# ff2 by seven block products in 12 of 16 chunks, with half of ff1's low parts from an accumulating transfer

## The chip, the cores and the metric

One core of a Trainium2 chip runs the kernel. The metric is the device time of one execution in microseconds. The engines named here: PE (matmuls), DVE (elementwise), ACT (activations, casts), POOL, and the queues that issue transfers, SP's and POOL's among them. Each works through its own list of instructions in order and waits on the others by semaphores.

## The reference, cut to what matters

One decoder layer on 256 tokens of width 1024, all in float32: a token mixer, then an MLP with squared ReLU, then a final norm. The change touches only the MLP:

```
h = rms_norm(x, norm_mlp)
u = square(relu(h @ w_ff1))     # w_ff1: 1024 x 4096
x = x + u @ w_ff2               # w_ff2: 4096 x 1024
return rms_norm(x, norm_final)
```

## The kernel before, in words

The kernel hands PE operands in a rounded format (`F32R`), so each float32 operand is split into a high part (`hi`, the rounded value) and a low part (`lo`, what is left), and each product is three matmuls: hi x hi, hi x lo, lo x hi (`mm3`). `split` (L70) does it: ACT casts to `hi`, DVE subtracts to get `lo`.

The weights come in chunks of 128 x 2048 floats (1 MB). `load` (L89) issues the transfer of a chunk into one of three `raw` buffers from SP's queue; `split_w` (L96) splits it, half by half, into one of four buffers for high parts (`wh`) and one of four for low parts (`wl`), and after the second half issues the load three chunks ahead. The hidden width 4096 is cut into NF = 16 groups j. Group j has one ff1 chunk (1024 x 256 of w_ff1) and one ff2 chunk (256 x 1024 of w_ff2); the chunks alternate: ff2's j, ff1's j+2, and so on.

`ff1` (L785) makes the 256 hidden values of a group for all 256 tokens in one PSUM bank: 2 halves x 8 steps over the width x 3 = 48 matmuls of 256 columns. `ff1_out` and `ff1_evac` (L772) then make r = relu (ACT), uh = r squared as high part (ACT), u = r squared (DVE), ul = u - uh (DVE). `ff2_mm` (L797) multiplies: a group's u is a 2 x 2 arrangement of 128 x 128 blocks (two halves kk of the hidden values, two halves t of the tokens), its ff2 chunk a 2 x 2 arrangement of 128 x 512 blocks (kk, and n for two halves of the output). Four banks `facc[t, n]` collect all groups; each group adds 2 kk x 4 (t, n) x 3 = 24 matmuls of 512 columns.

The whole program is one hand-written order: each engine issues its instructions as the code emits them. Until the MLP, a list of slots with a `plan` of side steps gives the order. Then a loop over j (L916) emits: ff2 of group j; the splits of the next ff1 chunk; ff1 of group j+2; the splits of the next ff2 chunk; the evacuation of group j+2. I call one pass of it a turn. The last two groups are left to a tail: `last_mm` (L942) runs both for one piece of the output after another, and the final norm and the stores follow piece by piece.

Of the kernel before, what the change touches and what calls it, by code (L numbers as in the profile page):

```python
# [32 lines left out]
def trunk_kernel(ctx: ExitStack, tc, x, x_t, w_in, w_out, w_ff1, w_ff2, small, hg_norm, norm_final, out):  # L33
    nc = tc.nc
    V, A, G, T = nc.vector, nc.scalar, nc.gpsimd, nc.tensor

    const = ctx.enter_context(tc.tile_pool(name="const", bufs=1))
    RAW = 3
    raw_p = ctx.enter_context(tc.tile_pool(name="raw", bufs=RAW))
    spl_p = ctx.enter_context(tc.tile_pool(name="spl", bufs=4))  # L40
# [38 lines left out]
    NF = 16  # L79
    chunks = [w_in[c] for c, _ in in_order] + [w_out[j] for j in range(4)]  # L80
# [536 lines left out]
    ps_s, sc_t, nm_t, pr_t, ps_t, PT = {}, {}, {}, {}, {}, {}  # L617
# [145 lines left out]
    FI = NI + 4  # L763
    uh, ul = {}, {}

    def ff1_mm(o, i, c, k):
        wh = hi_w[i].rearrange("p (k c) -> p k c", c=CW)
        wl = lo_w[i].rearrange("p (k c) -> p k c", c=CW)
        cs = slice(c * 128, (c + 1) * 128)
        mm3(o, (wh[:, k, cs], wl[:, k, cs]), (x1h[:, k, :], x1l[:, k, :]), k == 0, k == KT - 1)  # L770
# [12 lines left out]
    ff1_ps = {}  # L783

    def ff1(j, i):  # L785
        ps = ff1_ps[j] = mis(f"f{j}")
        for c in range(2):
            for k in range(KT):
                ff1_mm(ps[:, c * 256:(c + 1) * 256], i, c, k)

    def ff1_out(j):
        ff1_evac(j, [(ff1_ps[j], slice(0, 512))])
        free(f"f{j}")

    facc = {}

    def ff2_mm(j, i, kk, t, n):  # L797
        if j == 0 and kk == 0:
            facc[t, n] = mis(f"fo{t}{n}")
        cs = slice(kk * 256 + t * 128, kk * 256 + (t + 1) * 128)  # L800
        big_mm(facc[t, n], uh[j][:, cs], ul[j][:, cs], i, kk, n, j == 0 and kk == 0,
               (t, n) == (1, 1) and j == NF - 3 and kk == 1)

    f0 = {}

    def ff1_first(c, kg):
# [106 lines left out]
    i = FI + 2  # L913
# [150 lines left out]
```

## Time and profile before

| | us |
|---|---|
| median of 3 runs (lowest, highest) | 320.41 (320.21, 321.88) |
| the profiled execution | 320.52 |
| its span | 318.8 |
| PE / DVE / ACT busy in the span | 309.5 / 191.9 / 171.9 |

The span runs from the first to the last instruction of the profile; the execution's own time lies 1.7 us above it. Matmuls overlap in the records (each lasts longer than its distance to the next), so PE's prices are read from start to start.

### The profile page before, as it was taken

To read this page: it belongs to the slowest core of one execution; us is meant where nothing else is said; L and a number is where in the kernel's file an instruction comes from. 1 tells how busy PE (TensorE), PEld (TensorE's weight loads), DVE (VectorE), ACT (ScalarE), POOL (GpSimd) and SP (SyncE) were. 2 spreads that over 40 slices of the span, in tenths; PEclk is the share of its full clock that TensorE was granted. 3 is DMA by queue.
4 is the path that set the end of the run, shared out by engine and by line. 5 is a ranking of instruction groups with operands and counts; after the bars stand their busy time and mean duration, and the time that the engine had idled before them with its cause. 6 is when DMAs were issued, how large, how long until landed. Compare 5 with 4: busy or idle time off the path is not lost.

```text
span 318.8 us, 5290 instructions
## 1 busy us (share of the span) xinstructions
PE 309.5 (97%) x2164; PEld 283.4 (89%) x2164; DVE 191.9 (60%) x287; ACT 171.9 (54%) x283; POOL 34.2 (11%) x83
## 2 busy tenths in 40 slices
PE   7999999999999999999999999999999999999991
PEld 6999999998999888999899889889989988988881
DVE  1848999983545493697734743753573474366353
ACT  3869699684595460686632652562364265246131
POOL 8338600021410000000000000000000000000000
PEclk9999999999999999999999999999999999999997
DMA  7996553360046346058656246436525624630003
GB/s 202 411 387 229 177 222 132 134 243 23 2 148 249 133 141 257 0 199 329 217 246 255 88 185 264 140 125 265 205 85 238 263 85 181 263 134 1 0 5 129
DMA packets 9961, 55.71 MB, mean 175 GB/s; under 512 B 1232, under 2 KB 1488, under 8 KB 4048
## 3 DMA queue, kind: packets, MB, share of 16 engines
q1 hardware_dynamic: 9216, 54.06, 45.1%
q10 hardware_dynamic: 720, 1.31, 1.3%
q8 instruction: 17, 0.28, 0.3%
q14 instruction: 8, 0.07, 0.1%
HBM read 54.32 MB, written 1.05 MB: 174 GB/s over the span
## 4 chain that ended last, share of the span: by engine, by line
PE 87%; DVE 5%; ACT 2%; DMA 2%; issue 2%; POOLq 0%; POOL 0%; DVEq 0%; ACTq 0%
PE banks L301 26%; PE banks L303 26%; PE banks L302 26%; DVE wl L72 2%; DMA raw<-in_w_in_dram 2%; PE banks L405 2%; ACT wh L71 1%; PE banks L641 1%; PE banks L659 1%; PE banks L168 1%; PE banks L676 1%; PE banks L675 1%; PE banks L458 1%; PE banks L521 1%; PE banks L674 1%
## 5 line engine op out<-in xcount | busy, mean ns | idle before, releaser
L72 DVE TENSOR_TENSOR wl<-raw,wh 128x1024 fp32r<-128x1024 f32 (+1 forms) x100 | 113.8, 1184 | 19.3 <-ACT wh L71 17.7
L71 ACT CAST wh<-raw 128x1024 fp32r<-128x1024 f32 (+1 forms) x100 | 95.3, 1009 | 3.3 <-DMA raw<-in_w_in_dram 3.3
L301 PE MATMUL banks<-x1h,wh 128*128 128x256 f32 x256 | 72.4, 283 | 0.0
L302 PE MATMUL banks<-x1l,wh 128*128 128x256 f32 x256 | 72.4, 283 | 0.0
L303 PE MATMUL banks<-x1h,wl 128*128 128x256 f32 x256 | 72.4, 283 | 0.0
L778 ACT ACTIVATE fr<-banks 128x512 f32<-128x512 f32 (+1 forms) x17 | 9.7, 573 | 87.2 <-PE banks L303 87.2
L780 DVE TENSOR_TENSOR fu<-fr 128x512 f32<-128x512 f32 (+1 forms) x17 | 11.2, 659 | 69.5 <-ACT fr L778 69.5
L303 PE MATMUL banks<-wh,ul 128*128 128x512 f32 (+1 forms) x132 | 51.4, 390 | 0.1
L301 PE MATMUL banks<-wh,uh 128*128 128x512 f32 (+1 forms) x132 | 51.4, 390 | 0.0
L302 PE MATMUL banks<-wl,uh 128*128 128x512 f32 (+1 forms) x132 | 51.4, 389 | 0.0
L301 PEld LDWEIGHTS banks<-x1h,wh 128*128 128x128 f32 x256 | 49.0, 191 | 0.7
L302 PEld LDWEIGHTS banks<-x1l,wh 128*128 128x128 f32 x256 | 48.9, 191 | 0.7
L303 PEld LDWEIGHTS banks<-x1h,wl 128*128 128x128 f32 x256 | 49.0, 191 | 0.0
L301 PE MATMUL banks<-hTh,wh 128*128 128x256 f32 x128 | 37.5, 293 | 0.3 <-ACT hTh L161 0.3
L302 PE MATMUL banks<-hTl,wh 128*128 128x256 f32 x128 | 36.4, 284 | 0.7 <-DVE hTl L162 0.7
L303 PE MATMUL banks<-hTh,wl 128*128 128x256 f32 x128 | 36.3, 283 | 0.0
L303 PEld LDWEIGHTS banks<-wh,ul 128*128 128x128 f32 x132 | 24.8, 188 | 6.2 <-DVE ul L781 0.6
L301 PEld LDWEIGHTS banks<-wh,uh 128*128 128x128 f32 x132 | 24.9, 189 | 5.4 <-ACT uh L779 0.4
L302 PEld LDWEIGHTS banks<-wl,uh 128*128 128x128 f32 x132 | 24.9, 188 | 5.0
L302 PEld LDWEIGHTS banks<-hTl,wh 128*128 128x128 f32 x128 | 24.5, 191 | 1.2 <-DVE hTl L162 1.1
L301 PEld LDWEIGHTS banks<-hTh,wh 128*128 128x128 f32 x128 | 24.5, 191 | 1.2 <-ACT hTh L161 0.7
L303 PEld LDWEIGHTS banks<-hTh,wl 128*128 128x128 f32 x128 | 24.5, 191 | 0.2 <-DVE wl L72 0.2
(198 smaller groups left out, 412.9 us busy)
## 6 DMA issues: line engine op xcount, KB each, us to landing
raw<-in_w_ff_dram SPq DMA_DIRECT2D x32, 1024.0 KB, 5.1
raw<-in_w_in_dram SPq DMA_DIRECT2D x10, 1024.0 KB, 5.7
raw<-in_w_out_dram SPq DMA_DIRECT2D x4, 1024.0 KB, 4.8
raw<-in_w_in_dram ACTq DMA_DIRECT2D x4, 256.0 KB, 7.1
xtok<-in_x_dram SPq DMA_DIRECT2D x2, 512.0 KB, 8.0
xa<-in_x_dram SPq DMA_DIRECT2D x2, 512.0 KB, 6.2
xa<-in_x_t_dram SPq DMA_DIRECT2D x3, 256.0 KB, 6.2
raw<-in_w_in_dram SPq DMA_DIRECT2D x2, 256.0 KB, 8.0
```

Source lines behind the costliest of these rows:

```text
L71: A.copy(hi, src)
L72: V.tensor_tensor(lo, src, hi.bitcast(F32), op=OP.subtract)
L168: T.transpose(pair[n % 2][:, i * 256 + t * 128:i * 256 + (t + 1) * 128], src[:, t, (k0 + n) * P:(k0 + n + 1) * P], ident)
L301: T.matmul(o, lh, rh, start=first, stop=False)
L302: T.matmul(o, lh, rl, start=False, stop=False)
L303: T.matmul(o, ll, rh, start=False, stop=last)
L405: T.matmul(ps[:, par, g * 64:(g + 1) * 64], kB[r, hp, hs], rhs, start=True, stop=True)
L458: T.matmul(dst, att_d[:, (hp * 2 + half) * 2 + par, :], bv[:, half, h * 64:h * 64 + 64], start=True, stop=(half == 0))
L521: T.matmul(ps[:, c * 256:(c + 1) * 256], spw[:, wofs + c * 128:wofs + (c + 1) * 128], xc[:, c, :], start=True, stop=True)
L641: T.matmul(ps_s[2 * pair + par][:, os], q[r, c, qs], k[r, c, ks], start=True, stop=True)
L778: A.activation(r[:, s_], src, AF.Relu)
L780: V.tensor_tensor(u[:, s_], r[:, s_], r[:, s_], op=OP.mult)
```

## The change

For groups 0 to 11 (NS = 12) ff2 is done by seven products of blocks instead of eight (a scheme of Strassen's kind). The blocks of u are combined into S1 to S4 and those of the weights into T1 to T4 by additions. Each of the seven products collects its sum over the 12 groups in a PSUM bank of its own, and `ff2_merge` adds the seven sums into the residual x, scaled by the norm's factors, after group 11. Groups 12 to 15 go as before, with four banks opened at group 12.

`ws_first` splits the three weight blocks that are used as they are, `ws_second` makes the four combinations in one buffer `tw` and splits them. `us_split` replaces `ff1_evac` for these groups and also makes S1 to S4 and their two parts.

For the ff1 chunks of groups 3 to 13, `w1_neg` prepares the second half (steps 4 to 7 over the width) in another way: ACT writes the rounded negative of the weights into the low part and again into the high part, and a transfer of 512 KB from POOL's queue adds the chunk from memory onto the first: what is left is the low part. The high part is then negative, and `ff1_mm` multiplies it with the negative of x1 (`nx`, made once by `x1_neg`). The first half is split as before.

The order of the loop changes: ff2 of group j; evacuation of group j+1; the splits for ff2 of group j+1 around those of ff1 of group j+3; ff1 of group j+2. The split of chunk 17 moves from slot 83 to slots 74 and 76. In the tail, the first output pieces take group 14 for both, then group 15 for both.

```diff
+        xh, xl = x1h[:, k, :], x1l[:, k, :]
+        if i in neg and k >= 4:
+            xh, xl = nx[:, 0, k - 4, :], nx[:, 1, k - 4, :]
+        T.matmul(o, wh[:, k, cs], xh, start=k == 0, stop=False)
+        T.matmul(o, wh[:, k, cs], xl, start=False, stop=False)
+        T.matmul(o, wl[:, k, cs], x1h[:, k, :], start=False, stop=k == KT - 1)
...
+    NS = 12
+    tw = wt("tw", [P, 2048], tag="yTl")
+    blk = [slice(b * 512, (b + 1) * 512) for b in range(4)]
+    lo2, hi2 = slice(0, 1024), slice(1024, 2048)
+    def x1_neg():
+        for b, src in enumerate((x1h, x1l)):
+            A.activation(flat(nx[:, b]), flat(src[:, 4:8, :]).bitcast(F32), AF.Copy, scale=-1.0)
+    def w1_neg(i):
...
+        A.activation(lo_w[i][:, hi2], raw[i][:, hi2], AF.Copy, scale=-1.0)
+        A.activation(hi_w[i][:, hi2], raw[i][:, hi2], AF.Copy, scale=-1.0)
+        nc.gpsimd.dma_start(lo_w[i][:, hi2], chunks[i][:, hi2], accum_op=OP.add)
+        split(hi_w[i][:, lo2], lo_w[i][:, lo2], raw[i][:, lo2])
+    def ws_first(i):
...
+        for s_ in (blk[0], hi2):
+            split(hb[:, s_], lb_[:, s_], R[:, s_])
+    def ws_second(i):
...
+        V.tensor_tensor(tw[:, lo2].rearrange("p (a c) -> p a c", a=2),
+                        R.rearrange("p (a b c) -> p a b c", a=2, b=2)[:, :, 1, :],
+                        R[:, lo2].rearrange("p (a c) -> p a c", a=2), op=OP.subtract)
+        V.tensor_tensor(tw[:, blk[2]], R[:, blk[3]], tw[:, blk[0]], op=OP.subtract)
+        A.copy(ht[:, lo2], tw[:, lo2])
+        V.tensor_tensor(tw[:, blk[3]], tw[:, blk[2]], R[:, blk[2]], op=OP.subtract)
+        A.copy(ht[:, hi2], tw[:, hi2])
+        V.tensor_tensor(lt, tw, ht.bitcast(F32), op=OP.subtract)
+        load(i + RAW)
+    def us_split(j, parts):
...
+        for src, s_ in parts:
+            A.activation(r[:, s_], src, AF.Relu)
+        A.activation(u, r, AF.Square)
+        A.activation(uh[j], r, AF.Square)
+        V.tensor_tensor(S1, A21, A22, op=OP.add)
+        V.tensor_tensor(S2, S1, A11, op=OP.subtract)
+        V.tensor_tensor(S3, A11, A21, op=OP.subtract)
+        V.tensor_tensor(S4, A12, S2, op=OP.subtract)
+        A.copy(sh[j], d)
+        V.tensor_tensor(ul[j], u, uh[j].bitcast(F32), op=OP.subtract)
+        V.tensor_tensor(sl[j], d, sh[j].bitcast(F32), op=OP.subtract)
+    def ff2_s(j, i):
+        for m in (1, 2, 3, 5, 7, 6, 4):
...
+            mm3(pacc[m], (h[j][:, cs], l[j][:, cs]), sb[i][m], j == 0, j == NS - 1)
+    def ff2_merge():
...
+        A.copy(p1, pacc[1])
+        into(0, 0, pacc[2], r2)
+        V.tensor_tensor(u2, p1, pacc[6], op=OP.add)
+        V.tensor_tensor(u3, u2, pacc[7], op=OP.add)
+        V.tensor_tensor(u4, u2, pacc[5], op=OP.add)
+        into(0, 1, pacc[3], r2)
+        into(1, 1, pacc[5], r2)
+        into(1, 0, pacc[4], nr2)
+        into(0, 0, p1, r2)
+        into(0, 1, u4, r2)
+        into(1, 0, u3, r2)
+        into(1, 1, u3, r2)
...
+        74: [(S_, 17, 0)],
+        76: [(S_, 17, 1)],
-        83: [(S_, 17, 0), (S_, 17, 1)],
...
+    ws_first(FI + 2)
+    ws_second(FI + 2)
     ff1_first_out()
-    S_(FI + 2, 0)
-    S_(FI + 2, 1)
     ff1(1, FI + 1)
-    S_(FI + 3, 0)
-    S_(FI + 3, 1)
-    ff1_out(1)
+    w1_split(2)
+    x1_neg()
     x1_ss()
...
     for j in range(NF):
-        if j < NF - 2:
+        i = FI + 2 + 2 * j if j < NF - 1 else NCH - 1
+        if j < NS:
+            ff2_s(j, i)
+        elif j < NF - 2:
             for kk in range(2):
                 for t, n in tnt:
                     ff2_mm(j, i, kk, t, n)
         else:
             tail[j] = i
-        split_w(i + 2, 0)
-        split_w(i + 2, 1)
-        i += 1
-        if j + 2 < NF:
-            ff1(j + 2, i)
-            split_w(i + 2, 0)
-            split_w(i + 2, 1)
-            ff1_out(j + 2)
-            i += 1
+        if j + 1 < NF:
+            ff1_out(j + 1)
+        if j == NS - 1:
+            ff2_merge()
+        if j + 1 < NS:
+            ws_first(i + 2)
+            w1_neg(i + 3)
+            ws_second(i + 2)
+            load(i + 3 + RAW)
+            ff1(j + 2, i + 1)
+        elif j + 1 < NF:
+            i2 = min(i + 2, NCH - 1)
+            split_w(i2, 0)
+            split_w(i2, 1)
+            if j + 2 < NF:
+                ff1(j + 2, i + 1)
+                w1_split(j + 3)
...
-    for t, s_ in ((0, H0), (0, H1), (1, H0), (1, Q2), (1, Q3)):
-        last_mm(t, s_)
+    for j in tail:
+        for s_ in (H0, H1):
+            last_mm(0, s_, [j])
+    for s_ in (H0, Q2, Q3):
+        last_mm(1, s_, list(tail))
```

## Rows read from the trace of the kernel before

**Rows 1.** The page, part 1: busy us, share of the span, instructions.
```profile
PE 309.5 (97%) x2164; PEld 283.4 (89%) x2164; DVE 191.9 (60%) x287; ACT 171.9 (54%) x283; POOL 34.2 (11%) x83
```
**Rows 2.** The page, part 4: the chain that ended last, by engine.
```profile
PE 87%; DVE 5%; ACT 2%; DMA 2%; issue 2%; POOLq 0%; POOL 0%; DVEq 0%; ACTq 0%
```
**Rows 3.** Stage table, one turn: PE, PEld, DVE, ACT, POOL busy, clock, DMA.
```profile
175.62:186.97 11.35, 11.35 (x73) 10.26 (x72) 6.02 (x6) 5.01 (x6) 0.00 (x0) 1.00 0.48 182
```
**Rows 4.** Timeline of PE, 175 to 190: start, us, engine, line, operation.
```profile
175.42 0.39 PE L301 MATMUL banks<-wh,uh 128*128 128x512 f32 x1
...
181.03 0.28 PE L301 MATMUL banks<-x1h,wh 128*128 128x256 f32 x1
...
186.78 0.39 PE L301 MATMUL banks<-wh,uh 128*128 128x512 f32 x1
```
**Rows 5.** Timeline of ACT, one turn; in brackets idle time before.
```profile
175.62 0.60 ACT L778 ACTIVATE fr<-banks 128x512 f32<-128x512 f32 x1 [6.30 <-PE banks L303]
176.25 0.63 ACT L779 ACTIVATE uh<-fr 128x512 fp32r<-128x512 f32 x1
176.78 3.88 ACT L71 CAST wh<-raw 128x1024 fp32r<-128x1024 f32 x4
186.97 0.60 ACT L778 ACTIVATE fr<-banks 128x512 f32<-128x512 f32 x1 [6.31 <-PE banks L303]
```
**Rows 6.** Timeline of DVE, the same turn.
```profile
176.25 0.69 DVE L780 TENSOR_TENSOR fu<-fr 128x512 f32<-128x512 f32 x1 [5.12 <-ACT fr L778]
177.04 0.69 DVE L781 TENSOR_TENSOR ul<-fu,uh 128x512 fp32r<-128x512 f32 x1
177.85 4.63 DVE L72 TENSOR_TENSOR wl<-raw,wh 128x1024 fp32r<-128x1024 f32 x4
```
**Rows 7.** Groups by line and shape from 140 us on: busy us, mean ns.
```profile
L72 DVE TENSOR_TENSOR wl<-raw,wh 128x1024 fp32r<-128x1024 f32 x59 | 68.3, 1219 | 2.1 <-ACT wh L71 0.6
L71 ACT CAST wh<-raw 128x1024 fp32r<-128x1024 f32 x57 | 55.4, 1043 | 0.0
L956 DVE SCALAR_TENSOR_TENSOR xa<-banks,r,xa 128x512 f32<-128x512 f32 x4 | 3.0, 750 | 3.1 <-PE banks L303 3.1
```
**Rows 8.** Timeline of DVE ahead of the loop over groups.
```profile
125.50 0.69 DVE L746 TENSOR_TENSOR xa<-xa,banks 128x512 f32<-128x512 f32 x1 [2.04 <-PE banks L303]
...
137.85 0.42 DVE L781 TENSOR_TENSOR ul<-fu,uh 128x256 fp32r<-128x256 f32 x1
```
**Rows 9.** Timeline of ACT ahead of the loop and in its first turn.
```profile
132.36 0.87 ACT L175 ACTIVATE x1h<-banks,xa 128x256 fp32r<-128x256 f32 x2 [0.19 <-DVE x1l L176]
...
142.71 1.05 ACT L819 ACTIVATE sq<-xa 128x1024 f32<-128x1024 f32 x1
...
144.93 3.88 ACT L71 CAST wh<-raw 128x1024 fp32r<-128x1024 f32 x4
152.90 0.60 ACT L778 ACTIVATE fr<-banks 128x512 f32<-128x512 f32 x1 [4.08 <-PE banks L303]
```
**Rows 10.** Waits from 150 us on: total us, times, longest.
```profile
PEld banks L303 <- DVE ul L781: 0.6, 1, 0.6
PEld banks L301 <- ACT uh L779: 0.4, 1, 0.4
```
**Rows 11.** Loads of weight chunks from 140 to 250 us, issue to landing.
```profile
DMA to landing us min/median/max: 4.7/5.1/6.6
```
**Rows 12.** Transfers by line: count, KB each, median us to landing.
```profile
xtok<-in_x_dram SPq DMA_DIRECT2D x2, 512.0 KB, 8.0
```
**Rows 13.** Waits of POOL: total us, times, longest.
```profile
POOL r L973 <- DVE v L969: 202.7, 2, 198.2
```
**Rows 14.** Stage table, the end, columns as in rows 3.
```profile
312.00:314.00 2.00, 0.39 (x4) 0.19 (x2) 1.23 (x5) 0.11 (x2) 0.35 (x1) 1.00 0.07 27
314.00:316.00 2.00, 0.00 (x0) 0.00 (x0) 0.88 (x2) 0.72 (x1) 0.20 (x1) 0.84 0.21 69
316.00:318.80 2.80, 0.00 (x0) 0.00 (x0) 0.00 (x0) 0.00 (x0) 0.00 (x0) 0.50 0.39 138
```

More of the change, by code (lines that the diff above doesn't have):

```diff
@@ L769, in ff1_mm @@
         cs = slice(c * 128, (c + 1) * 128)
-        mm3(o, (wh[:, k, cs], wl[:, k, cs]), (x1h[:, k, :], x1l[:, k, :]), k == 0, k == KT - 1)
+        xh, xl = x1h[:, k, :], x1l[:, k, :]
[4 more added lines that the diff above has]
+        T.matmul(o, wl[:, k, cs], x1h[:, k, :], start=False, stop=k == KT - 1)
     def ff1_evac(j, parts):
@@ L791, in ff1_out @@
     def ff1_out(j):
-        ff1_evac(j, [(ff1_ps[j], slice(0, 512))])
+        (us_split if j < NS else ff1_evac)(j, [(ff1_ps[j], slice(0, 512))])
         free(f"f{j}")
+    NS = 12
+    sb, sh, sl, pacc = {}, {}, {}, {}
+    tw = wt("tw", [P, 2048], tag="yTl")
+    blk = [slice(b * 512, (b + 1) * 512) for b in range(4)]
+    lo2, hi2 = slice(0, 1024), slice(1024, 2048)
+    nx = wt("nx", [P, 2, 4, 256], tag="yTh", dt=F32R)
+    neg = set()
+    def x1_neg():
+        for b, src in enumerate((x1h, x1l)):
+            A.activation(flat(nx[:, b]), flat(src[:, 4:8, :]).bitcast(F32), AF.Copy, scale=-1.0)
@@ new lines, in w1_neg @@
+    def w1_neg(i):
+        hi_w[i] = spl_p.tile([P, 2048], F32R, name=f"wh{i}", tag="wh")
+        lo_w[i] = spl_p.tile([P, 2048], F32R, name=f"wl{i}", tag="wl")
+        neg.add(i)
+        A.activation(lo_w[i][:, hi2], raw[i][:, hi2], AF.Copy, scale=-1.0)
[3 more added lines that the diff above has]
+    def ws_first(i):
+        R = raw[i]
+        hb = spl_p.tile([P, 2048], F32R, name=f"wh{i}", tag="wh")
+        lb_ = spl_p.tile([P, 2048], F32R, name=f"wl{i}", tag="wl")
+        for s_ in (blk[0], hi2):
+            split(hb[:, s_], lb_[:, s_], R[:, s_])
+        B11, B21, B22 = [(hb[:, blk[b]], lb_[:, blk[b]]) for b in (0, 2, 3)]
+        sb[i] = {1: B11, 2: B21, 3: B22}
@@ new lines, in ws_second @@
+    def ws_second(i):
+        R = raw[i]
+        ht = spl_p.tile([P, 2048], F32R, name=f"wh{i}t", tag="wh")
+        lt = spl_p.tile([P, 2048], F32R, name=f"wl{i}t", tag="wl")
+        V.tensor_tensor(tw[:, lo2].rearrange("p (a c) -> p a c", a=2),
[7 more added lines that the diff above has]
+        load(i + RAW)
+        T1, T3, T2, T4 = [(ht[:, blk[b]], lt[:, blk[b]]) for b in range(4)]
+        sb[i].update({5: T1, 7: T3, 6: T2, 4: T4})
@@ new lines, in us_split @@
+    def us_split(j, parts):
+        r = wt("fr", [P, 512], tag="sc", bufs=3)
+        u = wt("fu", [P, 512], tag="pr", bufs=2)
+        d = wt("fs", [P, 512], tag="sc", bufs=3)
+        uh[j], ul[j], sh[j], sl[j] = [wt(n, [P, 512], tag="PT", bufs=8, dt=F32R) for n in ("uh", "ul", "sh", "sl")]
+        for src, s_ in parts:
+            A.activation(r[:, s_], src, AF.Relu)
+        A.activation(u, r, AF.Square)
+        A.activation(uh[j], r, AF.Square)
+        A11, A21, A12, A22 = [u[:, b * 128:(b + 1) * 128] for b in range(4)]
+        S1, S2, S3, S4 = [d[:, b * 128:(b + 1) * 128] for b in range(4)]
+        V.tensor_tensor(S1, A21, A22, op=OP.add)
[5 more added lines that the diff above has]
+        V.tensor_tensor(sl[j], d, sh[j].bitcast(F32), op=OP.subtract)
@@ new lines, in ff2_s, with into @@
+    def ff2_s(j, i):
+        for m in (1, 2, 3, 5, 7, 6, 4):
+            if j == 0:
+                pacc[m] = mis(f"P{m}")
+            h, l, b = {1: (uh, ul, 0), 2: (uh, ul, 2), 4: (uh, ul, 3), 5: (sh, sl, 0), 6: (sh, sl, 1),
+                       7: (sh, sl, 2), 3: (sh, sl, 3)}[m]
+            cs = slice(b * 128, (b + 1) * 128)
+            mm3(pacc[m], (h[j][:, cs], l[j][:, cs]), sb[i][m], j == 0, j == NS - 1)
+    def ff2_merge():
+        p1, u2, u3, u4 = [wt(n, [P, 512], tag=g) for n, g in (("p1", "qc"), ("u2", "kB"), ("u3", "sig_f"),
+                                                                 ("u4", "qk"))]
+        def into(t, n, src, r):
+            s_ = slice(n * 512, (n + 1) * 512)
+            V.scalar_tensor_tensor(xt[:, t, s_], src, r[:, t:t + 1], xt[:, t, s_], op0=OP.mult, op1=OP.add)
+        A.copy(p1, pacc[1])
+        free("P1")
+        into(0, 0, pacc[2], r2)
+        free("P2")
+        V.tensor_tensor(u2, p1, pacc[6], op=OP.add)
+        free("P6")
+        V.tensor_tensor(u3, u2, pacc[7], op=OP.add)
+        free("P7")
+        V.tensor_tensor(u4, u2, pacc[5], op=OP.add)
+        into(0, 1, pacc[3], r2)
+        free("P3")
+        into(1, 1, pacc[5], r2)
+        free("P5")
+        into(1, 0, pacc[4], nr2)
+        free("P4")
+        into(0, 0, p1, r2)
+        into(0, 1, u4, r2)
+        into(1, 0, u3, r2)
+        into(1, 1, u3, r2)
@@ L795, in trunk_kernel @@
     facc = {}
     def ff2_mm(j, i, kk, t, n):
-        if j == 0 and kk == 0:
+        if j == NS and kk == 0:
             facc[t, n] = mis(f"fo{t}{n}")
         cs = slice(kk * 256 + t * 128, kk * 256 + (t + 1) * 128)
-        big_mm(facc[t, n], uh[j][:, cs], ul[j][:, cs], i, kk, n, j == 0 and kk == 0,
+        big_mm(facc[t, n], uh[j][:, cs], ul[j][:, cs], i, kk, n, j == NS and kk == 0,
                (t, n) == (1, 1) and j == NF - 3 and kk == 1)
@@ L812, in ff1_first_out @@
     def ff1_first_out():
-        ff1_evac(0, [(f0[c], slice(c * 256, (c + 1) * 256)) for c in range(2)])
+        us_split(0, [(f0[c], slice(c * 256, (c + 1) * 256)) for c in range(2)])
         free("f00")
@@ L821, in x1_ss @@
         V.reciprocal(r2, ss2[:, 0, :])
+        V.tensor_scalar(nr2, r2, -1.0, None, op0=OP.mult)
     r2 = wt("r2", [P, 2])
+    nr2 = wt("nr2", [P, 2])
     nfb = wt("nfb", [P, D], tag="oc")
@@ L903, in trunk_kernel, with w1_split @@
         slot[0](*slot[1:])
+    def w1_split(j):
+        if j < NF:
+            split_w(FI + 1 + 2 * j - 2, 0)
+            split_w(FI + 1 + 2 * j - 2, 1)
+    ws_first(FI + 2)
+    ws_second(FI + 2)
     ff1_first_out()
-    S_(FI + 2, 0)
-    S_(FI + 2, 1)
     ff1(1, FI + 1)
-    S_(FI + 3, 0)
-    S_(FI + 3, 1)
-    ff1_out(1)
+    w1_split(2)
+    x1_neg()
     x1_ss()
     nc.sync.dma_start(nfb, bass.AP(tensor=norm_final.tensor, offset=norm_final.offset, ap=[[0, P], [1, D]]))
-    i = FI + 2
     tnt = sorted(tn)
@@ L940, in trunk_kernel, with last_mm @@
     own = {}
-    def last_mm(t, s_):
+    def last_mm(t, s_, js):
         fresh = t == 1 and s_ in (Q2, Q3)
-        if fresh:
+        if fresh and NF - 2 in js:
             own[t, s_.start] = mis(f"fq{s_.start}")[:, 0:256]
         o = own[t, s_.start] if fresh else facc[t, s_.start // 512]
-        for j, i in tail.items():
+        for j in js:
+            i = tail[j]
             for kk in range(2):
```

## The prediction

> **What bounds the kernel now.** I read the page's busy shares first: PE is busy 97% of the span, DVE 60%, ACT 54% [rows 1]. The chain of waits agrees: 87% of it is PE, and three lines of matmuls carry it [rows 2]. The stage table shows the same in the stretch that the change rewrites: in one turn of the MLP loop (11.35 us) PE is busy all of it, DVE 6.02 us and ACT 5.01 us [rows 3]. So a matmul removed there is worth its full spacing, as long as DVE and ACT stay inside the shorter turn.
>
> The PE timeline gives the prices. A ff2 block runs from 175.42 to 181.03, 24 matmuls of 512 columns: 5.61 / 24 = 0.234 us each. A ff1 block runs from 181.03 to 186.78, 48 of 256 columns: 0.120 us each, 5.75 us. A turn is 11.36 us [rows 4].
>
> ACT and DVE do their work in one burst and then wait: ACT 6.31 us for PE, DVE 5.12 us for ACT [rows 5, 6]. These waits hide everything that they do now. I price their operations from here. ACT: 512 columns last 0.60 to 0.63 us and 1024 last 1.04; the next one starts 0.53 and 0.95 us later if it needs nothing fresh (four casts take 3.88) [rows 5, 7]. DVE: 1.22 us for 1024, 0.69 for 512, 0.42 for 256, so 0.53 more per 512 columns: 2.28 for 2048, 0.29 for 128; independent ones follow 0.08 us before the end (four take 4.63, so 1.14 each) [rows 6 to 8]. A result on the same engine or the other is picked up 0.03 us after its end (fr ends at 176.22, uh and fu start at 176.25), or 0.10 after when two things are waited for (fu ends at 176.94, ul starts at 177.04) [rows 5, 6].
>
> **The change, part by part.** *PE.* Seven products of three matmuls are 21 instead of 24 in each of 12 chunks: 36 x 0.234 = 8.4 us less. The turn would be 21 x 0.234 + 5.75 = 10.66 us.
>
> *ACT and DVE.* Each engine issues in the order written, so I add the turn in that order. ACT per turn: r, u, uh, sh (512 each), the casts of block 0 (512) and of the second half (1024), two negations and one cast of ff1's chunk (1024 each), two casts of the differences (1024 each): 5 x 0.53 + 6 x 0.95 = 8.4 us, against 5.0 now. DVE: S1 to S4, ul, sl, three low parts (512, 1024, 1024), three differences (1024, 512, 512), one low part of 2048: 1.1 + 5 x 0.61 + 3 x 1.14 + 2.2 = 9.8, against 6.0. Each sum is below 10.66. But they hand work to and fro, and neither can pass its own queue. The loop through both queues, from the big low part of one chunk to that of the next, is:
>
> lt (2048, DVE) 2.20; S1 to S4 behind it in DVE's queue, S2 and S4 on fresh results, 1.10; ACT can only now do sh, then block 0: 2 x 0.53 = 1.06; the second half and the two negations 3 x 0.95 = 2.85; the cast of ff1's first half 1.07; DVE its low part 1.14 and, only behind it, the differences 1.25 + 0.72 + 0.72; ACT the cast of the second pair 1.07; then lt again. Sum 13.18 us. r, u and uh lie beside lt and cost nothing here; if lt were shorter than their 1.8 us, they would be next.
>
> So the turn is not PE's 10.66 but about 13.3 (I add 0.1 for steps that wait for two things; six such at 0.07 make 13.6 the upper end; S and the differences at independent intervals make 12.6 the lower). PE then sits idle some 2.6 us per turn ahead of the fourth product, whose differences' low part comes last. The negations take 1.14 us of DVE's work away and put 0.95 more on ACT, in the same loop: they buy about 0.2.
>
> VectorE's row for 1024 columns is 1.219 us, and a dependent one starts 0.03 us after that [rows 6, 7]. [...]
>
> *Start.* The split of ff2's first chunk now stands ahead of the evacuation of ff1's first. ACT is done with the second norm's splits at 133.2 (132.36 + 0.87 [rows 9]), DVE soon after. From there: 0.53 + 1.07 + 1.14 + 1.25 + 0.72 + 0.72 + 1.07 + 2.28 = 142.0 for lt, then S and ul to 143.5. Before, fr of ff1's third block starts at 152.90 [rows 9]; that block took 5.75 and ff2's first 5.61, so PE is free for ff2 at 141.5: 2.0 idle, and the shorter block ends at 148.4. Chunk 17's split moves forward into a gap of the projection (DVE waits 2.04 us there [rows 8]), without cost; it needs 2.3, so an addition behind it could slip by 0.3. The seven products hold seven banks, so ff1 has one: it can start only when r has emptied it. ACT does two casts (1.9), the new negations of x1 (1.9) and the two sums of squares (2.2, from 142.71 to 144.93 now [rows 9]) first: r starts at 149.5, PE idles 1.7 us to 150.1. From r at 149.5 the loop's steps give lt at 164.1 (0.65 + 0.65 for r and u, then 13.2), so the second block ends at 164.1 + 4 x 0.70 = 166.9. Before, ff2's second block ended 5.6 us after 152.90, at 158.5: +8.4.
>
> *Ten more turns:* 10 x (13.3 - 11.36) = +19.4.
>
> *End.* The merge puts seven reads of banks at 0.67 (such a read of 512 columns lasts 0.75 [rows 7]) and four adds at 0.61 into DVE's queue ahead of the low parts of the next ff2 chunk: 7.1 us, of which about 1.4 can run before the block's last product. With the low part of 1.22 behind it, it is done about 7.0 us after the block, and ff1's 5.75 cover all but 1.2: +1.2 (between 0, ff1 covering all, and 2.6, the merge starting at the block's end). The tail's new order puts 12 matmuls ahead of the last u, where PE waited 0.6 + 0.4 [rows 10]; the last chunk's split now comes behind that evacuation and leaves 0.75: -0.25.
>
> *Transfers.* SP issues the next two loads when the third difference has read its buffer. The first is needed by the negations 6.4 us later (1.07 + 2.20 + 1.10 + 1.06 + 0.95), and lands in 4.7 to 6.6, median 5.1 [rows 11]: hidden, by a little over 1 us. If a second load 0.3 us behind it stretches it to the 8.0 of the crowded start [rows 12], 1.6 to 1.9 per turn come on top. The accumulating transfer has no row. It goes through POOL's queue, where nothing else stands in this stretch (POOL waits 198.2 us in one piece [rows 13]). Its result is needed by a ff1 block about 12.5 us after its issue. Nearest rows: 1 MB lands in 4.7 at best, 512 KB at the crowded start in 8.0 [rows 11, 12]; if it must read its destination too, twice 8.0 would add 3.5 per turn, +38. I take 8.0 and no cost: half the bytes of the loads, read twice, are nearest to these.
>
> *Buffers.* Four split buffers serve three new tiles per turn. If the differences get the one that ff1's block still reads, their first cast waits for that block, which ends 2.8 + 5.75 = 8.55 us behind lt; in the loop it comes 8.5 us behind lt. Nothing to 0.1 per turn.
>
> **Sum.** +8.4 + 19.4 + 1.2 - 0.25 = +28.7. The profiled execution took 320.52 us, 1.7 outside its span of 318.8, and lies 0.1 from the median of 320.41. 320.5 + 28.7 = 349.2; I predict 349.
>
> **Rivals.**
> *A: faster, PE stays the bound.* If ACT and DVE overlap better than their queues' order says, the turn is 10.66: 320.5 - 8.4 + 3.7 (start) + 1.2 - 0.25 = 317. For it: each engine's sum is under PE's. Against it: the steps of the loop are results that the next one reads, or stand behind it in a queue. It decides at a loop of 11.36, where gain and loss meet.
> [...]
>
> *B: slower still, transfers late.* The load of ff1's chunk lands after 8 us instead of 5.1: ten or eleven turns of 1.6 to 1.9 more, 366 to 370; at the longest row of 6.6, +0.5 per turn, 355. For it: both loads are issued together, and 0.5 MB more per turn moves. Against: 2.5 MB in 13.3 us is 190 GB/s, and the stretch moves 182 now [rows 3].
>
> [...]
>
> **How the numbers follow.** The forecast, a loop of 12.6 to 13.6: 0.74, 342 to 354. B: 0.12, 354 to 370. A: 0.09, 312 to 318. A loop between A's and mine: 0.02. C in every turn, or a slow accumulating transfer: 0.03. Below 340 lies some 0.11, above 364 some 0.08: the range is 340 to 364. Faster by over 0.5%, about what can be told from no change here: 0.09; within: 0.01; slower: 0.90.
>
> **What would show it.** Right: ff2 turns of 13.3 us; PE waiting about 2.6 us in each for the DVE low part of the differences, at the fourth product; hardly an ACT wait for PE; DVE waiting for ACT's casts; 36 matmuls fewer. [...] If DVE's 2048-column low part is not what the fourth product waits for, the loop is wrong.

## The result, and the profile after

The changed kernel takes 349.47 us (median of 4 runs, 349.01 to 349.92); the kernel before takes 320.51 beside it. The ratio is 1.090, its interval 1.088 to 1.092: slower, by the 29 us that were forecast. The profiled execution took 349.92 us, 1.7 outside its span.

The page after, part 1 (busy us, share of the span, instructions), the row of the granted clock in part 2 (tenths of full speed in 40 slices), and part 4, the chain that ended last:
```profile
PE 313.9 (90%) x2128; PEld 283.3 (81%) x2128; DVE 248.7 (71%) x382; ACT 217.3 (62%) x344; POOL 44.3 (13%) x94
PEclk9999999999999999998799899899999899899997
PE 37%; DVE 31%; ACT 23%; issue 4%; DMA 2%; POOLq 0%; POOL 0%; DVEq 0%; ACTq 0%
```
Beside [rows 1, 2]: 36 matmuls are gone, PE's share fell from 97 to 90%, and its share of the chain from 87 to 37%. DVE and ACT together now carry 54% of the chain, though neither is busy for more than 71% of the span. That fits a loop through two queues, in which each engine waits for the other.

ACT of the changed kernel, one turn (start, us, operation; in brackets idle time before and who ended it). L862 is sh, L71 the casts, L817 and L818 the negations, L839 and L841 the casts of the differences:
```profile
213.30 1.05 ACT L841 CAST wh28t<-tw 128x1024 fp32r<-128x1024 f32 x1 [0.34 <-DVE tw L840]
...
217.64 0.62 ACT L862 CAST sh<-fs 128x512 fp32r<-128x512 f32 x1 [1.62 <-DVE fs L861]
218.17 1.56 ACT L71 CAST wh<-raw 128x512 fp32r<-128x512 f32 x2
219.63 1.05 ACT L817 ACTIVATE wl<-raw 128x1024 fp32r<-128x1024 f32 x1
220.59 1.04 ACT L818 ACTIVATE wh<-raw 128x1024 fp32r<-128x1024 f32 x1
221.54 1.03 ACT L71 CAST wh<-raw 128x1024 fp32r<-128x1024 f32 x1
225.05 1.05 ACT L839 CAST wh30t<-tw 128x1024 fp32r<-128x1024 f32 x1 [2.48 <-DVE tw L835]
226.44 1.05 ACT L841 CAST wh30t<-tw 128x1024 fp32r<-128x1024 f32 x1 [0.34 <-DVE tw L840]
```
DVE in the same turn. L842 is the big low part, L858 the first of S1 to S4, L835 to L840 the differences:
```profile
214.38 2.29 DVE L842 TENSOR_TENSOR wl28t<-tw,wh28t 128x2048 fp32r<-128x2048 f32 x1 [1.12 <-ACT wh28t L841]
216.59 0.28 DVE L858 TENSOR_TENSOR fs<-fu 128x128 f32<-128x128 f32 x1
...
222.60 1.23 DVE L72 TENSOR_TENSOR wl<-raw,wh 128x1024 fp32r<-128x1024 f32 x1 [1.62 <-ACT wh L71]
223.74 1.22 DVE L835 TENSOR_TENSOR tw<-raw 128x1024 f32<-128x1024 f32 x1
224.99 0.69 DVE L838 TENSOR_TENSOR tw<-raw,tw 128x512 f32<-128x512 f32 x1
225.72 0.69 DVE L840 TENSOR_TENSOR tw<-tw,raw 128x512 f32<-128x512 f32 x1
227.53 2.29 DVE L842 TENSOR_TENSOR wl30t<-tw,wh30t 128x2048 fp32r<-128x2048 f32 x1 [1.12 <-ACT wh30t L841]
```
Follow the starts from one L842 to the next: 214.38 (DVE), 216.59 (DVE), 217.64 (ACT), 218.17, 219.63, 220.59, 221.54 (ACT), 222.60, 223.74, 224.99, 225.72 (DVE), 226.44 (ACT), 227.53 (DVE). Together 13.15 us, against 11.36 before [rows 4]. The waits in brackets are no longer waits for PE, as in [rows 5], but the two engines' waits for each other: 1.62 + 2.48 + 0.34 on ACT, 1.12 + 1.62 on DVE.

PE of the changed kernel, around the second matmul of the fourth product in five turns, the loop's second, sixth, seventh, ninth and last:
```profile
164.12 0.79 PE L302 MATMUL banks<-wl20t,sh 128*128 128x512 f32 x1 [3.23 <-DVE wl20t L842]
164.71 0.63 PE L303 MATMUL banks<-wh20t,sl 128*128 128x512 f32 x1
165.13 0.63 PE L301 MATMUL banks<-wh20t,sh 128*128 128x512 f32 x1
...
216.73 0.50 PE L302 MATMUL banks<-wl28t,sh 128*128 128x512 f32 x1 [2.26 <-DVE wl28t L842]
217.07 0.39 PE L303 MATMUL banks<-wh28t,sl 128*128 128x512 f32 x1
...
218.42 0.63 PE L302 MATMUL banks<-wl28t,sh 128*128 128x512 f32 x1
218.85 0.63 PE L303 MATMUL banks<-wh28t,sl 128*128 128x512 f32 x1
...
229.87 0.50 PE L302 MATMUL banks<-wl30t,sh 128*128 128x512 f32 x1 [0.71 <-DVE wl30t L842]
...
256.18 0.50 PE L302 MATMUL banks<-wl34t,sh 128*128 128x512 f32 x1 [2.26 <-DVE wl34t L842]
...
295.62 0.50 PE L302 MATMUL banks<-wl40t,sh 128*128 128x512 f32 x1 [2.25 <-DVE wl40t L842]
```
PE waits for the big low part at the place that was named: 3.2 us in the second turn, 2.0 to 2.3 us in six others, 0.7 to 0.8 us in three (the one for `wl30t` is such), and not at all in the third. After the pause at 216.73 its matmuls start 0.43 us apart for a while, not 0.23: the granted clock is 0.50 from 218 to 220 us. In the turn behind such a stretch PE comes late itself, and its wait is the short one. The stage table (two stretches of about a turn each; length, busy us of PE, PEld, DVE, ACT, POOL, clock, DMA share, GB/s) shows what that does:
```profile
205.60:218.80 13.20, 10.94 (x69) 9.66 (x68) 10.09 (x14) 8.72 (x13) 0.87 (x1) 0.97 0.62 197
218.80:232.00 13.20, 12.49 (x72) 10.91 (x71) 10.11 (x14) 8.73 (x12) 0.88 (x1) 0.90 0.65 202
```
PE is busy 10.9 us in one stretch and 12.5 in the next, for nearly the same matmuls (a turn has 69). DVE's 10.1 and ACT's 8.7 are the same in both (in [rows 3] 6.0 and 5.0). No engine fills the turn.

### The profile page after: what moved, and what is told of

It is laid out like the page before. It is cut to its first block, busy times and chain, and to the rows that moved or that the text cites. A ratio compares the mean times of both kernels' runs of the same rounds, so it can differ in the third digit from the quotient of the medians.

```text
span 348.2 us, 5421 instructions
## 1 busy us (share of the span) xinstructions
PE 313.9 (90%) x2128; PEld 283.3 (81%) x2128; DVE 248.7 (71%) x382; ACT 217.3 (62%) x344; POOL 44.3 (13%) x94
## 3 DMA queue, kind: packets, MB, share of 16 engines
HBM read 60.08 MB, written 1.05 MB: 176 GB/s over the span
## 4 chain that ended last, share of the span: by engine, by line
PE 37%; DVE 31%; ACT 23%; issue 4%; DMA 2%; POOLq 0%; POOL 0%; DVEq 0%; ACTq 0%
ACT wh L71 10%; PE banks L302 9%; PE banks L301 9%; PE banks L303 8%; DVE wl L72 7%; DVE tw L835 4%; ACT wl L817 3%; ACT wh L818 3%; DVE tw L838 2%; DVE tw L840 2%; DMA raw<-in_w_in_dram 2%; PE banks L405 2%; PE banks L775 1%; PE banks L773 1%; PE banks L774 1%
## 5 line engine op out<-in xcount | busy, mean ns | idle before, releaser
L72 DVE TENSOR_TENSOR wl<-raw,wh 128x1024 fp32r<-128x1024 f32 (+1 forms) x89 | 97.2, 1110 | 37.2 <-ACT wh L71 37.0
L71 ACT CAST wh<-raw 128x1024 fp32r<-128x1024 f32 (+1 forms) x89 | 81.0, 946 | 7.6 <-DMA raw<-in_w_ff_dram 4.4
L773 PE MATMUL banks<-x1h,wh 128*128 128x256 f32 x168 | 48.2, 287 | 1.9 <-ACT fr L853 1.9
L774 PE MATMUL banks<-x1l,wh 128*128 128x256 f32 x168 | 47.9, 285 | 0.0
L773 PEld LDWEIGHTS banks<-x1h,wh 128*128 128x128 f32 x168 | 32.9, 196 | 3.1 <-ACT fr L853 2.3
L774 PEld LDWEIGHTS banks<-x1l,wh 128*128 128x128 f32 x168 | 32.7, 194 | 0.8
L773 PE MATMUL banks<-nx,wh 128*128 128x256 f32 x88 | 24.9, 283 | 0.0
L774 PE MATMUL banks<-nx,wh 128*128 128x256 f32 x88 | 24.9, 283 | 0.0
L302 PE MATMUL banks<-wl,uh 128*128 128x512 f32 (+1 forms) x60 | 23.1, 385 | 1.3 <-DVE wl L72 1.3
L303 PE MATMUL banks<-wh,ul 128*128 128x512 f32 (+1 forms) x60 | 22.9, 382 | 1.4 <-DVE ul L863 1.4
L301 PE MATMUL banks<-wh,uh 128*128 128x512 f32 (+1 forms) x60 | 22.8, 380 | 0.0
L301 PE MATMUL banks<-wh,hTh 128*128 128x256 f32 x64 | 18.9, 296 | 0.0
L862 ACT CAST sh<-fs 128x512 fp32r<-128x512 f32 x12 | 7.4, 620 | 17.6 <-DVE fs L861 17.6
```

The lines of the kernel that those rows point to most:

```text
L773: T.matmul(o, wh[:, k, cs], xh, start=k == 0, stop=False)
L774: T.matmul(o, wh[:, k, cs], xl, start=False, stop=False)
```

## The experiments

The theory: the turn is the loop of dependent steps through ACT's and DVE's queues. The rivals: the sum of work of one engine sets it; PE sets it, by its work or its clock; the transfers do.

**PE's work taken away.** Each block product loses its third matmul (the low part of the activations' side), 84 in all:
```diff
-            mm3(pacc[m], (h[j][:, cs], l[j][:, cs]), sb[i][m], j == 0, j == NS - 1)
+            T.matmul(pacc[m], h[j][:, cs], sb[i][m][0], start=j == 0, stop=False)
+            T.matmul(pacc[m], h[j][:, cs], sb[i][m][1], start=False, stop=j == NS - 1)
```


> The third matmul of each of the seven products is left out (low part of u times high part of the weights), so PE has 7 x 12 = 84 matmuls less, 19.7 us; nothing else changes. Loop theory: PE is off the path of the turns, and the time moves by 0 to -3 us (start and end only). Rival, PE or its clock sets the turn: 330 or less.

Measured 348.88 us, ratio 1.087 (1.085 to 1.090). Its page, part 1:
```profile
PE 302.8 (87%) x2044; PEld 274.4 (79%) x2044; DVE 248.8 (71%) x382; ACT 217.2 (62%) x344; POOL 44.3 (13%) x94
```
84 matmuls are worth 19.7 us at 0.234 each; the time moved by 0.6. PE's work is off the path. The mean granted clock fell to 0.935 (0.965 in the changed kernel) and that cost nothing either: neither PE's work nor its clock sets the turn. By busy share PE comes first in the changed kernel (90% for its matmuls, 81% for its weight loads, 71% for DVE), and still work taken from it moves next to nothing.

**The same subtraction at two places.** A spare DVE subtraction of 1024 columns into a scratch tile, in each of eleven turns, once where DVE waits for ACT's sums, once between ff1's low part and the differences:
```diff
     # e5_hidden: behind the low part of ff2's second half
+        if i > FI + 2:
+            V.tensor_tensor(sq2, R[:, lo2], R[:, hi2], op=OP.subtract)
     # e6_on_path: behind the low part of ff1's chunk
+        V.tensor_tensor(sq2, raw[i][:, lo2], raw[i][:, hi2], op=OP.subtract)
```


> One spare VectorE subtraction of 1024 columns is added to each of ten turns, into a scratch tile, right behind the low part of ff2's second half, where VectorE waits 1.62 us for ScalarE's sums in the changed kernel's trace; the same instruction stands in expectation e6_on_path at another place. By the theory of the loop through both queues the spare 1.14 us is waited away there anyway: turn 13.15 as before, time 349 to 350 us (at most 351.5 if the small instructions behind it slip by 0.1 to 0.2 a turn). By the rival that VectorE's sum of work sets the turn (it has the longest list of the two queues) ten times 1.14 is added: 361 us.

> The same spare VectorE subtraction of 1024 columns, but behind ff1's low part of the next chunk, ahead of the three second sums that ScalarE waits for; eleven of them. By the loop theory it lies on the loop: eleven times 1.14 is 12.5, time 361 to 363 us. By the rival that only sums of work count, the two places cost the same: whatever e5_hidden shows. If TensorE or the transfers set the turn, neither costs anything: 349.5.

Measured 349.85 us (349.12 to 350.44) and 362.28 us (361.43 to 363.75). DVE of the first, the spare at L829 and the big low part at L844:
```profile
221.31 1.22 DVE L829 TENSOR_TENSOR sq<-raw 128x1024 f32<-128x1024 f32 x1
223.00 1.23 DVE L72 TENSOR_TENSOR wl<-raw,wh 128x1024 fp32r<-128x1024 f32 x1 [0.48 <-ACT wh L71]
...
227.93 2.29 DVE L844 TENSOR_TENSOR wl30t<-tw,wh30t 128x2048 fp32r<-128x2048 f32 x1 [1.11 <-ACT wh30t L843]
```
DVE of the second, the big low part at L843 in two turns:
```profile
206.40 2.29 DVE L843 TENSOR_TENSOR wl26t<-tw,wh26t 128x2048 fp32r<-128x2048 f32 x1 [1.12 <-ACT wh26t L842]
...
220.68 2.29 DVE L843 TENSOR_TENSOR wl28t<-tw,wh28t 128x2048 fp32r<-128x2048 f32 x1 [1.11 <-ACT wh28t L842]
```
At the first place DVE's wait for ACT shrinks from 1.62 to 0.48, by the 1.14 that the subtraction takes, and the turn stays at 13.14 (the big low part starts at 214.79 and 227.93). At the second the turn is 14.28, 1.13 more, and the time 12.8 more. The first expectation speaks of ten turns, but the edit puts the subtraction into eleven: both pages count 393 DVE instructions, against 382 in the changed kernel. So eleven such instructions cost 0.4 us, which lies within the spread of the runs, or 12.8, by where they stand. The sum-of-work rival falls: DVE does the same work in both.

**The big low part in two halves.**
```diff
-        V.tensor_tensor(lt, tw, ht.bitcast(F32), op=OP.subtract)
+        for s_ in (lo2, hi2):
+            V.tensor_tensor(lt[:, s_], tw[:, s_], ht[:, s_].bitcast(F32), op=OP.subtract)
```


> Only the low part of the differences, one subtraction of 2048 columns, is done as two of 1024, the first behind the first cast. Loop theory: the first half lies beside the second cast (1.07), so the loop loses 1.07 + 2.20 - 2.28 = 1.0 us per turn, though DVE has 0.08 us more to do: 11 turns, 338 to 339. Rival, sum of work: 350 (+0.08 per turn). Rival, a late transfer or PE's clock: 349.5, unchanged.

Measured 336.5 us, ratio 1.050 (1.047 to 1.052). Its DVE, the halves at L843:
```profile
208.44 2.42 DVE L843 TENSOR_TENSOR wl28t<-tw,wh28t 128x1024 fp32r<-128x1024 f32 x2
...
220.56 2.42 DVE L843 TENSOR_TENSOR wl30t<-tw,wh30t 128x1024 fp32r<-128x1024 f32 x2
```
DVE works 0.13 us more per turn (2.42 for 2.29), and the turn is 1.03 shorter, 12.12: the first half no longer waits for ACT's second cast. It came out 1.5 to 2.5 us better than expected. The expectation left out two things: PE's fourth product now waits for the first half alone, and PE's clock stays up: in its profile the granted clock is 0.992 over the span and 1.00 from 205.6 to 232 us, against 0.965 and 0.90 to 0.97 in the changed kernel.

**Without the accumulating transfer.** ff1's chunk is split as before, with no negations:
```diff
-        neg.add(i)
-        A.activation(lo_w[i][:, hi2], raw[i][:, hi2], AF.Copy, scale=-1.0)
-        A.activation(hi_w[i][:, hi2], raw[i][:, hi2], AF.Copy, scale=-1.0)
-        nc.gpsimd.dma_start(lo_w[i][:, hi2], chunks[i][:, hi2], accum_op=OP.add)
-        split(hi_w[i][:, lo2], lo_w[i][:, lo2], raw[i][:, lo2])
+        for s_ in (lo2, hi2):
+            split(hi_w[i][:, s_], lo_w[i][:, s_], raw[i][:, s_])
...
-    x1_neg()
```


> No accumulating transfer and no negations: both halves of ff1's chunk are split by ACT and DVE as before the change, first half first; the negation of x1 is gone. DVE has 1.14 us more per turn, ACT 0.95 less. The prediction's step said that the negations buy about 0.2 us per turn: then 351.5. Loop theory with the order read closely: behind the second half stand c (1.07), then DVE's two low parts (1.14 each, the second cast beside the first), 3.35, where n1, n2, c and one low part took 4.11: 0.76 less per turn, and 1.9 less at the start: 349.5 - 8.4 - 1.9 = 339 to 341. Rival, DVE's sum of work sets the turn: +1.14 per turn, 362. Rival, the accumulating transfer is late or in the way of the loads: 349.5 less more than 10.

Measured 340.81 us, ratio 1.063 (1.061 to 1.065). Its DVE, the big low part at L839:
```profile
209.60 2.29 DVE L839 TENSOR_TENSOR wl28t<-tw,wh28t 128x2048 fp32r<-128x2048 f32 x1 [1.12 <-ACT wh28t L838]
...
214.98 3.50 DVE L72 TENSOR_TENSOR wl<-raw,wh 128x1024 fp32r<-128x1024 f32 x3 [0.18 <-ACT wh L71]
...
222.17 2.29 DVE L839 TENSOR_TENSOR wl30t<-tw,wh30t 128x2048 fp32r<-128x2048 f32 x1 [1.11 <-ACT wh30t L838]
```
Turn 12.57. Three low parts stand back to back and DVE does not wait between them. In the changed kernel the same stretch of the loop is ACT's two negations and a cast, 2.97 us (219.63 to 222.60), with DVE idle for 1.62 of it. So the transfer and its negations cost 8.7 us in this order: 0.58 in each of ten turns, and 2.65 ahead of them, where the second turn's big low part starts at 159.12 instead of 161.77; most of that is the negations of the input (1.9 us in ACT's queue).

**Six chunks instead of twelve.**
```diff
-    NS = 12
+    NS = 6
```


> Six of ff2's chunks by seven block products instead of twelve; chunks 7 to 12 go as in the kernel before. By the loop theory each turn undone gives back 13.15 less 11.36, six times 1.8 is 10.7: 338.8 us, range 337 to 341, and the 8.4 us of the start stay. By the rival that the start and the merge of the seven products carry most of the loss, under 4 us is given back: 345 to 349. The turns that remain are to show 13.1 to 13.2, and those behind them 11.3 to 11.4.

Measured 339.32 us (338.66 to 339.50): 10.15 us given back for 10.7 expected. Its ACT behind the sixth chunk, fr of two turns:
```profile
249.81 0.60 ACT L783 ACTIVATE fr<-banks 128x512 f32<-128x512 f32 x1 [6.28 <-PE banks L775]
...
261.14 0.60 ACT L783 ACTIVATE fr<-banks 128x512 f32<-128x512 f32 x1 [6.27 <-PE banks L775]
```
From there the turns are 11.33 again, and ACT waits for PE as in [rows 5]. The loss goes with the number of turns.

**The same instructions in another order.** Inside the turn only: the differences first, on DVE while ACT empties the bank of ff1; then r, u, uh, all casts of raw chunks and sh on ACT; the casts of the differences and the negations last. The core of it, the order within the new function told in comments:
```diff
-            ws_first(i + 2)
-            w1_neg(i + 3)
-            ws_second(i + 2)
+            turn(j + 1, i + 2)
+            # DVE: differences, S1 to S4, ff2's low parts, ul, ff1's low part, sl, lt
+            # ACT: r, u, uh, ff2's casts, ff1's cast, sh, casts of the differences, negations
+            # POOL: the accumulating transfer, last
```


> The same instructions as the changed kernel, inside a turn in another order: the three differences first in DVE's queue, r, u, uh, block 0, the second half and ff1's first half first in ACT's, the casts of the differences ahead of the two negations, and the big low part last in DVE's. Loop theory: no step waits round both queues any more, DVE's own sum of 9.8 to 10.1 us fits into PE's 10.66, so the turn falls from 13.15 to about 10.7; the first turn gains some 4 us, ten more 2.5 each: 349.5 - 28 = 321, between 317 and 326. Rival, amount of work or of transfers (all of it is unchanged) sets the turn: 345 to 350. Rival, PE's lower clock sets it: PE still pauses, 340 or more.

Measured 323.48 us, ratio 1.009 (1.006 to 1.012). Its ACT, fr of two turns, and PE's worst wait:
```profile
226.26 0.60 ACT L1031 ACTIVATE fr<-banks 128x512 f32<-128x512 f32 x1 [1.85 <-PE banks L775]
...
236.91 0.60 ACT L1031 ACTIVATE fr<-banks 128x512 f32<-128x512 f32 x1 [1.83 <-PE banks L775]
```
```profile
167.20 0.39 PE L775 MATMUL banks<-x1h,wl 128*128 128x256 f32 x1 [2.14 <-DMA wl<-in_w_ff_dram]
```
The turn is 10.65, PE's own, and ACT waits for PE again: order alone is worth 26 us (the loads of the next chunks are issued where their buffers have been read, and so move with it). What was missed: issued last, the accumulating transfer is late, and PE waits for it twice, together 3.8 us in the profiled execution, which at 326.06 us is the slowest of the six.

**That transfer issued early**, ahead of the casts of ff1's chunk, in the same order otherwise (the two added lines are moved up from the end of the turn; the expectation says ahead of the copies of ff2's chunk, but in the code they stand behind those):
```diff
         neg.add(n)
+        A.activation(lo_w[n][:, hi2], raw[n][:, hi2], AF.Copy, scale=-1.0)
+        nc.gpsimd.dma_start(lo_w[n][:, hi2], chunks[n][:, hi2], accum_op=OP.add)
         A.copy(hi_w[n][:, lo2], raw[n][:, lo2])
```


> As e1_order, with the negation and the accumulating transfer issued ahead of ScalarE's copies of ff2's chunk, and nothing of the other two edits of e8_best. e1_order is 11.1 us behind e8_best. By the theory that TensorE's waits add up, TensorE's two waits of together 3.8 us for this transfer go and the start's waits (1.4, 1.9 and 1.2 for the splits) and the split ahead of the merge stay: 318 to 320.5 us. By the rival that the late transfer alone keeps e1_order from its gain (each of its waits also takes the clock down for a stretch): 312 to 314. By the rival that the early issue does nothing, because the transfer lands 8 to 9 us after its issue wherever it is: 323.5.

Measured 319.90 us, ratio 0.9975 (0.996 to 0.999). PE's waits in it (total us, times, longest):
```profile
PE banks L302 <- DVE wl L72: 1.9, 3, 1.2
PE banks L773 <- ACT fr L1031: 1.9, 1, 1.9
...
PE banks L303 <- DVE ul L863: 1.4, 1, 1.4
```
The waits for the transfer are gone, and 3.6 us with them; so the late transfer alone is not what separates this order from its full gain. The waits of the start (1.9 for fr, 1.4 for ul) and the one of 1.2 behind the merge remain.

**A version that beats both.** To that order and transfer it adds: the split of ff2's first chunk in gaps of the stage ahead of the loop, the negations and sums of squares of the input in later turns, and the split that stood behind the merge in the merge's middle:
```diff
-        81: [(x1_add, 1, 1), (x1_tr, 4, 1), (x1_split, 4, 0), (x1_split, 4, 1)],
+        81: [(x1_add, 1, 1), (x1_tr, 4, 1), (w0_a,), (x1_split, 4, 0), (x1_split, 4, 1), (w0_b,)],
...
+        for h in range(2):                      # in the merge, behind its first reads
+            split_w(FI + 2 + 2 * NS, h)
...
-    ws_first(FI + 2)
-    ws_second(FI + 2)
...
-    x1_neg()
-    x1_ss()
```


> The order of e1_order inside the turn, with three more edits: the accumulating transfer is issued ahead of the copies of ff2's chunk (in e1_order it landed 8.3 us behind its issue and TensorE waited 3.8 us for it); the split of ff2's first chunk is taken out of the loop's start and put into gaps ahead of the last stage of the first feed-forward half's input (waits of 1.4 and 1.9 and two more in the start of the changed kernel); and the split that lies ahead of the merge of the products is put behind the merge's first reads. By the loop theory nothing of the two queues is late any more and TensorE sets the end: twelve chunks without 3 matmuls of 0.234 each give 8.4 us less than the kernel before: 320.5 less 8.4 is 312.1, with small waits 312 to 315, ratio 0.974 to 0.983. By the rival that the seven products can't pay in this kernel, because what they take off TensorE comes back as clock or as transfers: 319 to 324, as e1_order.

Measured 312.39 us (312.25 to 312.61), ratio 0.975 (0.973 to 0.976). Its page, parts 1 and 4, the one row of PE's waits from 150 us on, and the stage table of the stretch shown above:
```profile
PE 301.3 (97%) x2128; PEld 277.7 (89%) x2128; DVE 245.3 (79%) x382; ACT 214.7 (69%) x344; POOL 46.5 (15%) x94
PE 91%; DMA 2%; issue 2%; DVE 2%; ACT 1%; POOLq 0%; POOL 0%; ACTq 0%; DVEq 0%
```
```profile
PE banks L302 <- DVE wl L72: 0.7, 2, 0.5
```
```profile
205.60:218.80 13.20, 13.20 (x82) 11.79 (x81) 12.68 (x21) 11.02 (x16) 0.87 (x1) 1.00 0.89 269
218.80:232.00 13.20, 13.20 (x85) 11.91 (x84) 12.47 (x17) 11.05 (x15) 1.74 (x2) 1.00 0.75 237
```
As many matmuls as the changed kernel, busy 12.6 us less, mostly because the clock stays up (granted 0.995 over the span, against 0.965; in the changed kernel 50 matmuls from 164 us on start at about twice their usual distance, 0.43 us for 512 columns and 0.21 for 256, which is 9 us more), and PE never pauses in the loop. The gain over the kernel before is 8.1 us of the 8.4 that 36 matmuls are worth. Of the 7.5 us between the two last versions, the waits that went make up 4.5 (1.9, 1.4 and 1.2); from 145 to 158 us the granted clock is 1.00 here and 0.87 there, which bears on the rest. Start and merge were not tried apart.

Thirteen chunks in this version:

> As e8_best, with thirteen chunks by seven products. By the theory that TensorE sets the end, one more chunk without three matmuls takes 0.7 us off: 311.7 us, 311.2 to 312.4, ratio to the kernel before 0.971 to 0.975. By the rival that the merge is too late then (the last block's tail waits for the part that the merge adds, which the thirteenth chunk holds back), 1 to 3 us are added: 313 to 315.

Measured 312.08 us (311.98 to 312.10), ratio 0.973 (0.971 to 0.975): 0.3 less, of 0.7 expected. The intervals overlap, so the thirteenth chunk's gain is not settled; the merge-too-late rival of 313 to 315 is out.

## Why the prediction was right

*The loop.* Term by term, predicted and measured between starts in the turn above: lt 2.20, 2.21; S1 to S4 1.10, 1.05; sh, ff2's casts and the negations 3.91, 3.90; the cast of ff1's half 1.07, 1.06; its low part 1.14, 1.14; the differences 1.25 + 0.72 + 0.72, 1.25 + 0.73 + 0.72; their last cast 1.07, 1.09. Sum 13.18, 13.15. The 0.1 added for double waits was not needed. Durations from [rows 5 to 8] and the order in which each queue is written gave the turn to 0.03 us. Of the 2048-column form, which no row of before has, 2.28 was extrapolated and 2.29 measured.

*Start and turns.* The second turn's big low part was to end at 164.1, and PE starts on it at 164.12. Ten turns of 13.15 later PE starts on the last one at 295.62; with turns of 13.3 it would have been 297.1, so the ten turns together came out 1.5 us shorter than forecast. The eleven matmuls behind it, for which 2.8 us were reckoned with the one ahead of the wait, take 4.17 us, since PE's clock falls among them: 1.4 more. So the last of the twelve blocks ends at 299.79 (299.9 by the forecast). Against 271.9 in the trace of before that is 27.9; forecast 27.8. That these agree to 0.1 us is luck: two errors, −1.5 in the turns and +1.4 in the last block, cancel. The same clock loss stands behind the second turn's wait, where the next ff1 block starts at 168.97 instead of 166.9 (4.85 us for the eleven matmuls). The sum has no term for PE's clock; there its loss cost nothing in the end, since the next big low part starts 13.15 us behind the one before all the same (161.77, 174.92).

*The end.* +1.5 instead of +0.95, from PE's last matmuls: they start 41.7 us behind the twelfth block, 40.2 before. The wait behind the merge costs 0.8, not 1.2. The tail was to win 0.25 and loses 0.6: the last chunk's split, put behind the evacuation, makes PE late by 0.70 and 0.32 in place of the 0.12 and 0.29 of before. The prediction reads [rows 10] as 0.6 + 0.4 us of PE's waiting, but they are rows of the weight loads (PEld); PE itself was late by only 0.41 there. Sum: 27.9 + 1.5 = 29.4, the difference of the two profiled executions.

*The step that failed* is the one on the negations, "they buy about 0.2". They cost 0.58 per turn (13.15 against 12.57 without them), since they put 0.95 us more of ACT's on the loop at a place where, without them, DVE's low parts stand back to back. It was not in the sum, which priced the loop as it is, so the forecast did not suffer.

*Rivals.* A needed the queues to overlap; the order as written forbids it, and the reordered kernel shows that the same instructions can. PE became the bound again only there. B did not come: the loads landed after 6.1 us in the median, over the 5.1 of [rows 11] and inside the 6.4 of cover, and no negation in the loop waits for one; ACT's waits for loads, 4.4 us in all, lie behind the merge. The accumulating transfer, bounded by 8.0 and twice that, landed after 6.2. C, in the chances a loss in every turn, came in part: PE's matmuls of 512 columns start 0.43 us apart, not 0.23, behind five of the eleven big low parts (from 164, 190, 218, 269 and 296 us on). Four of these lie inside PE's slack of 2.5 us a turn: PE is busy 12.5 us of 13.2 in the one of the stage table. It cost only where the slack ended, in the last block (1.6 us by the price of 0.234 a matmul: 11 from 295.62 to 299.79).

*The price of a subtraction.* The row of 1.219 us for 1024 columns [rows 7] held: 1.22 in the changed kernel, and 2.29 for 2048.

From the after page and that of the best version, the landings (count, KB each, median us):
```profile
raw<-in_w_ff_dram SPq DMA_DIRECT2D x32, 1024.0 KB, 6.1
wl<-in_w_ff_dram POOLq DMA_DIRECT2D x11, 512.0 KB, 6.2
```
```profile
raw<-in_w_ff_dram SPq DMA_DIRECT2D x32, 1024.0 KB, 7.2
wl<-in_w_ff_dram POOLq DMA_DIRECT2D x11, 512.0 KB, 9.0
```

## What to carry to other kernels

Where two in-order queues hand work to and fro, walk the dependent steps from one turn to the same place in the next, in the order written, before believing the sums: 10.1, 8.7 and 10.7 us of work made a turn of 13.15 here, and the same instructions in another order one of 10.65. Before undoing a change that frees the bounding engine but comes out slower, reorder it: the work that waits for nothing first, the producer of what the other engine needs ahead of what it doesn't, transfers issued as soon as their source is there. To see whether an instruction is on the path, add one like it at its place and at the nearest wait; here it cost its own time at the one and next to nothing at the other.

## What the runs showed of the hardware

Pauses of the same length did not have the same effect on PE's clock. In the changed kernel PE pauses 2.26 us up to 216.73, and the granted clock is 1.00 through the pause; the next matmuls come 0.23 us apart, and 0.43 apart only from 217.99 on, 1.3 us after work was taken up. Behind the 2.25 us up to 295.62 the fall comes 0.8 us after, behind the 2.04 up to 190.42 and the 2.26 up to 269.33 the first matmuls are slow at once, as they are behind 2.10 and 3.23 us of pauses close together (160.40, 164.12). Behind the 2.27 us up to 243.02 and the 2.26 up to 256.18 it did not fall at all: the granted clock is 1.00 in the 5.8 us from each on. What decides this no run here shows. Where the clock fell behind a single pause, the matmuls took some 1.5 us more until it was back; so a pause can cost PE more than its length. In the reordered kernel with the late transfer the granted clock is 0.84 from 166 to 177 us, where the first of its two waits for the transfer lies (2.14 us up to 167.20); behind the second, 1.63 us up to 266.33, the matmuls of 256 columns stay 0.12 us apart: the clock did not fall there.

An accumulating transfer of 512 KB took longer to land in the faster kernels: 6.2 us at a DMA share of 0.62 to 0.65 in the loop, 9.0 at 0.75 to 0.89, where the 1 MB loads went from 6.1 to 7.2 (rows just above). The share alone does not tell it: from 177 to 300 us it is 0.73 in the reordered kernel with the late transfer, where the accumulating transfer landed after 8.3 us and the loads after 5.2, and 0.66 in the version with 9.0 and 7.2. No matmul waited for it while it was issued ahead of the casts of ff1's chunk.
